# A macaron layer on one core: where the chunk matrix is stored, who stores the state-space parameters, and how long a gated tile's turn waits

## The chip, the cores and the metric

The kernel runs on 1 core of one Trainium2 chip. The metric is the time of one execution on the device in microseconds (us). A core has a TensorE (PE) that multiplies matrices, a VectorE (DVE), a ScalarE (ACT) and a GpSimd (POOL) for elementwise work, and a SyncE (SP) that here only issues transfers. Transfers can be issued by SP, ACT and POOL, and are carried by 16 DMA engines.

## What is computed

One layer of a decoder trunk on 256 tokens of width 2048, in float32: a SwiGLU block of hidden width 5632 with half weight, then a mixer (dilated window attention beside a state-space model, S5, of 64 groups of 16 channels with 64 complex states each), then a second SwiGLU block.

```
for l in range(DEPTH):
    h = h + 0.5 * swiglu_ffn(rms_norm(h, ffn1_norm[l]), ffn1_w_gate[l], ffn1_w_up[l], ffn1_w_down[l])
    proj = rms_norm(h, mix_norm[l]) @ w_in[l]          # q | k | v | u
    attn = mixture_of_dilations(q, k, v, rel_bias)
    y = s5_ssm(u, ssm_lambda_re[l], ..., ssm_d[l])
    y = jax.nn.gelu(y)
    y = y * jax.nn.sigmoid(y @ glu_w[l] + glu_b[l])
    h = h + jnp.concatenate([attn, y], axis=-1) @ w_out[l]
    h = h + 0.5 * swiglu_ffn(rms_norm(h, ffn2_norm[l]), ffn2_w_gate[l], ffn2_w_up[l], ffn2_w_down[l])
```

The S5 recurrence is run in chunks of 8 tokens. Four sets of matrices, which depend on the parameters alone, are worked out while the first SwiGLU block runs: the chunk matrix `m1` (inputs of a chunk to its state), `m2` (state to outputs), `k` (one row of Toeplitz blocks) and from it `t` (inputs of a chunk to its outputs).

## The kernel before

**The weights.** All large products run in `run` (L252). A pass is one block of 512 output columns of a weight; a group of a pass is 512 rows of it, 1 MB, loaded by SP into one of three `raw` buffers (L273). Each group is split in two halves, and each half into a high part `wh` (ACT, L286) and a low part `wl` (DVE, L291), in four buffers each. One **step** is the 12 matmuls of 128x512 on one half (L330 to L332), after which `step()` lets every running generator go on to its next `yield`. So a step is the clock of all other work: a `yield n` waits n steps. Each engine and each queue carries out its instructions in the order in which they were written. The split written at a step is the one for three steps later, and a weight's load is written when a `raw` buffer has been split.

**The gated tile.** The first block has 11 tiles of 512 hidden columns, each a pass over `w_gate` and one over `w_up`, 8 steps each, and then four passes over `w_down`. When the two passes of a tile are done, ACT and DVE have made `silu(gate) * up` (L363, L374) in `sil`, tokens on partitions. It has to stand with hidden columns on partitions. `by_blocks` (L129) does this turn: DVE transposes blocks of 32x32 (L134), after a step SP stores them to DRAM (`h_d`, L137), after two more SP loads them back from there (L140, four loads of 32 partitions), and after `yield 3` the caller splits the tile with ACT (L124) and DVE (L125) into `hid`, which the `w_down` passes read.

**The parameters.** `ssm_prepare` (L422) is a generator beside the first block. After the recurrence's powers and coefficients it loops over four pieces `pc` of 16 groups each. For a piece it writes `m1t` (in `s4a`) and `wk` (in `slot3`) by eight calls of `powers` (L649), each three DVE instructions with a scratch `tmp2` in `s4b` (L655 to L657). Then POOL stores `wk` to `m2_d` in one transfer of 1 MB (L667), DVE transposes `m1t` into `m1o`, all of `s4b` (L670), POOL stores it to `m1_d` in one transfer of 1 MB (L673), PE makes `k` with 16 small matmuls (L679), and SP stores `k` with 4 transfers (L688) and copies it to `t_d`, DRAM to DRAM, with 8 (L691). The next piece follows at once. The buffers serve as `hid` tiles 5 to 10 later, so the turn of tile 5 and those after it wait until `ssm_prepare` has ended, and the gate pass of tile 7 does not begin before.

**The mixer.** Its first two passes make `u`. When the first is done, `u_done(0)` (L962) calls `load_m1` (L698), which writes 16 loads of `m1_d`, 256 KB to 32 partitions each, on SP's queue, one after another.

Of the kernel before, what the change touches and what calls it, by code (L numbers as in the profile page):

```python
# [16 lines left out]
P = 128  # L17
# [29 lines left out]
def hybrid_layer_kernel(  # L47
# [80 lines left out]

    def by_blocks(src, dst):  # L129
        turns[0] += 1  # L130
        b = const.tile([P, 4, NT, P], F32, name=nm("blocks"), tag="blocks")
        hd = h_d[turns[0] % 2]
        for t in range(NT):
            vec.transpose(out=b[:, :, t].rearrange("p j (k c) -> p j k c", k=4),  # L134
                          in_=src[:, t, :].rearrange("p (k j c) -> p j k c", k=4, j=4))
        yield
        sync.dma_start(out=hd.rearrange("j p x -> p j x"), in_=b.rearrange("p j t x -> p j (t x)"))  # L137
        yield 2
        for j in range(4):
            sync.dma_start(out=dst[32 * j:32 * j + 32].rearrange("r (i x) -> r i x", i=4),  # L140
                           in_=hd[j].rearrange("(i r) x -> r i x", i=4))
        yield 3
        return dst.rearrange("p (i t x) -> p i t x", i=4, t=NT)
# [194 lines left out]
    def ffn(norm, w_gate, w_up, w_down, done, first):  # L338
# [31 lines left out]
        def up_done(c):  # L370
            def f(acc):
                a = sil.pop(c)
                for t in range(NT):
                    vec.scalar_tensor_tensor(out=a[:, t, :], in0=acc[t], scalar=norm.scale(t),  # L374
                                             in1=a[:, t, :], op0=ALU.mult, op1=ALU.mult)
# [12 lines left out]
            return f  # L388
# [33 lines left out]
    def ssm_prepare():  # L422
# [23 lines left out]
        pool.dma_start(out=dpad[:, :, 0:16], in_=ssm_d[0].rearrange("(j q c) -> q j c", j=4, q=16))  # L446
        zer = s2a[:, 0:8 * 112].rearrange("p (t x) -> p t x", t=8)
        pool.memset(zer, 0.0)
# [3 lines left out]

        def expo(xa, new, res_):
            xc, n, f, e, p2, ex, em = (new() for _ in range(7))
# [111 lines left out]
        ptab = a3[:, 2816:3840].rearrange("p (k s g) -> p k s g", k=8, s=2)  # L566
        tmp2 = s4b[:, 1536:2048]
        coef = a3[:, 0:128].rearrange("p (s g) -> p s g", s=2)
# [50 lines left out]
        for v, dst in ((0, cs), (64, csw)):  # L619
            for hb in range(2):  # L620
# [4 lines left out]
                for i in range(4):  # L625
# [3 lines left out]
                                   func=AF.Copy, scale=sgn)  # L629
                yield  # L630
        ps = tps()
# [5 lines left out]
        vec.tensor_tensor(out=dmask, in0=dmask, in1=ident[:, 96:112], op=ALU.add)  # L637
        yield

# [3 lines left out]
        wk = a3[:, 0:2304].rearrange("p (g r c) -> p g r c", r=9, c=16)  # L643
        ko = a3[:, 2304:2816].rearrange("p (q x) -> p q x", q=4)
        for pc in range(4):
            gs = slice(16 * pc, 16 * pc + 16)
            es = slice(256 * pc, 256 * pc + 256)

            def powers(dst, k, n, z, sz, down=False):  # L649

                pr, pi = (ptab[:, k - 1:k - 1 + n, v, gs][:, ::-1 if down else 1].rearrange("p k g -> p g k")
                          .unsqueeze(3).broadcast_to([P, 16, n, 16]) for v in range(2))
# [4 lines left out]
                vec.tensor_tensor(out=dst, in0=dst, in1=t_, op=ALU.add)  # L657

            act.activation(out=m1t[:, :, 7, :], in_=g3(bb[:, es]), func=AF.Copy)
            act.activation(out=wk[:, :, 0, :], in_=g3(cs[:, es]), func=AF.Copy)  # L660
            for k in range(1, 9, 2):
                n = 2 if k < 7 else 1
                powers(m1t[:, :, 8 - k - n:8 - k, :], k, n, bb, sb, True)
                yield
                powers(wk[:, :, k:k + 2, :], k, 2, cs, csw)
                yield
            pool.dma_start(out=m2_d[pc].rearrange("p (g x) -> p g x", g=16),  # L667
                           in_=wk[:, :, 1:9, :].rearrange("p g r c -> p g (r c)"))
# [4 lines left out]
            pool.dma_start(out=m1_d[pc].rearrange("j p x -> p j x"), in_=m1o)  # L673
            yield
            ps = tps()
            for q in range(4):
                for j in range(4):
                    g = 16 * pc + 4 * q + j
                    pe.matmul(ps[32 * j:32 * j + 32, q * P:(q + 1) * P], s2a[:, 16 * g:16 * g + 32],  # L679
                              wk[:, 4 * q + j, 0:8, :].rearrange("p r c -> p (r c)"), start=True, stop=True)  # L680
            yield
            act.activation(out=ko, in_=ps.rearrange("p (q x) -> p q x", q=4), func=AF.Copy)
            for q in range(4):
                vec.scalar_tensor_tensor(out=ko[:, q, 0:16], in0=dmask, scalar=dcol[:, 4 * pc + q:4 * pc + q + 1],
                                         in1=ko[:, q, 0:16], op0=ALU.mult, op1=ALU.add)
            for j in range(4):
                dst = k_d.rearrange("(q j) c x -> j c q x", j=4)[j, :, 4 * pc:4 * pc + 4, 112:240]
                sync.dma_start(out=dst, in_=ko[32 * j:32 * j + 16])  # L688
            yield 2
            for r in range(CH):  # L690
                sync.dma_start(out=t_d[pc, 16 * r:16 * r + 16].rearrange("c (g x) -> c g x", g=16),  # L691
                               in_=k_d[16 * pc:16 * pc + 16, :, (7 - r) * 16:(7 - r) * 16 + P]
                               .rearrange("g c x -> c g x"))


    mx = {}

    def load_m1():  # L698
        r3 = slot("slot3")
        mx["ring"] = [slot("s2a"), slot("s2b"), r3[:, 0:2048], r3[:, 2048:4096]]  # L700
        for pc in range(4):
            for j in range(4):
                sync.dma_start(out=mx["ring"][pc][32 * j:32 * j + 32].rearrange("r (i x) -> r i x", i=4),
                               in_=m1_d[pc, j].rearrange("(i r) x -> r i x", i=4))

# [6 lines left out]
    def ssm_run():  # L712
# [248 lines left out]
    def mixer(norm, out_done):  # L961
        def u_done(n):  # L962
            def f(acc):
                if n == 0:
# [106 lines left out]
    with tc.manual_schedule():  # L1071
# [143 lines left out]
```

## Time and profile before

| | |
|---|---|
| time, three runs | 1836.66 us median (1832.95 to 1837.66) |
| the profiled execution | 1833.54 us, of which the span 1831.8 us |
| TensorE matmul busy | 1798.0 us of the span |
| VectorE busy | 1060.3 us |
| ScalarE busy | 834.7 us |
| DMA | 401.23 MB, mean 219 GB/s |

The span is what the profiler recorded from the first to the last instruction; the rest of the execution's time lies around it. Times "at 190 us" are counted from the span's start. In a row of a timeline an engine's idle time and what ended it stand in brackets. A matmul's recorded duration is its way through a pipeline: in an undisturbed stretch one of 128x512 starts every 0.23 us though its row says 0.39.

### The profile page before, as it was taken

Reading aid. Unit: us, or ns where it says so; the run is one execution under the profiler, and the core shown is the slowest. Engines: PE = TensorE matmul, PEld = TensorE weight load, DVE = VectorE, ACT = ScalarE, POOL = GpSimd, SP = SyncE. Lnnn points to the kernel's source line nnn. Section 1 sums busy time; section 2 is a strip of 40 time slices with the busy share of each in tenths; the row PEclk is TensorE's granted clock in tenths of the full one; section 3 lists DMA queues with packets and bytes.
Section 4 is the critical chain, followed back from the end, with each engine's and each line's share of the span. In section 5 each row is a group of like instructions: output and inputs, shape, how many; then the busy total and the mean of one; then the engine's idle time right before and its main releaser. Section 6 shows DMA issues by size and latency. Waiting matters only on the chain.

```text
span 1831.8 us, 21467 instructions
## 1 busy us (share of the span) xinstructions
PE 1798.0 (98%) x8389; PEld 1476.9 (81%) x8389; DVE 1060.3 (58%) x1382; ACT 834.7 (46%) x1071; POOL 43.4 (2%) x91
## 2 busy tenths in 40 slices
PE   8999999999999999989999999999999999999999
PEld 6788777788888888868878888888888888888887
DVE  4778788555554555534795665555555555544443
ACT  5444344444444444435667555444444444443332
POOL 2100000000000000010000001000000000000000
PEclk8999999999999999989999999999999999999999
DMA  8665788867776666599656586677767767665662
GB/s 270 208 213 191 254 264 283 262 211 213 224 218 215 209 219 216 186 255 302 186 156 250 197 246 212 195 232 217 224 212 217 219 210 225 208 222 202 202 211 103
DMA packets 220389, 401.23 MB, mean 219 GB/s; under 512 B 9580, under 2 KB 50133, under 8 KB 219136
## 3 DMA queue, kind: packets, MB, share of 16 engines
q1 hardware_dynamic: 214384, 383.29, 65.7%
q0 software_dynamic: 4080, 13.43, 2.4%
q10 hardware_dynamic: 1824, 3.15, 0.7%
q8 instruction: 65, 1.06, 0.2%
q14 instruction: 36, 0.29, 0.0%
HBM read 370.00 MB, written 32.45 MB: 220 GB/s over the span
## 4 chain that ended last, share of the span: by engine, by line
PE 84%; DVE 8%; DMA 5%; ACT 1%; issue 1%; SPq 1%; ACTq 0%; DVEq 0%
PE acc L330 27%; PE acc L331 27%; PE acc L332 27%; DVE wl L291 3%; DMA h_d<-blocks 2%; DMA sil<-h_d 1%; DMA raw<-in_ffn_w_gate_dram 1%; DVE s4b L655 1%; ACT wh L286 1%; DMA raw<-in_w_in_dram 1%; DVE s1a L768 1%; DVE s1a L769 0%; DVE slot L656 0%; DVE s4a L657 0%; DVE s4a L656 0%
## 5 line engine op out<-in xcount | busy, mean ns | idle before, releaser
L291 DVE TENSOR_TENSOR wl<-raw,wh 128x1024 fp32r<-128x1024 f32 x628 | 764.6, 1225 | 635.0 <-ACT wh L286 634.5
L286 ACT ACTIVATE wh<-raw 128x1024 fp32r<-128x1024 f32 (+1 forms) x636 | 666.2, 1057 | 820.6 <-PE acc L332 762.5
L330 PE MATMUL acc<-wh,xth 128*128 128x512 f32 x1664 | 658.7, 396 | 16.5 <-ACT wh L286 16.5
L331 PE MATMUL acc<-wl,xth 128*128 128x512 f32 x1664 | 653.9, 393 | 3.6 <-DVE wl L291 3.2
L332 PE MATMUL acc<-wh,xtl 128*128 128x512 f32 x1664 | 652.0, 392 | 0.0
L330 PEld LDWEIGHTS acc<-wh,xth 128*128 128x128 f32 x1664 | 314.9, 189 | 85.1 <-ACT wh L286 19.0
L331 PEld LDWEIGHTS acc<-wl,xth 128*128 128x128 f32 x1664 | 315.0, 189 | 74.0 <-DVE wl L291 9.7
L332 PEld LDWEIGHTS acc<-wh,xtl 128*128 128x128 f32 x1664 | 314.8, 189 | 66.1
L331 PE MATMUL acc<-wl,hid 128*128 128x512 f32 x704 | 274.0, 389 | 0.0
L330 PE MATMUL acc<-wh,hid 128*128 128x512 f32 x704 | 274.0, 389 | 0.0
L332 PE MATMUL acc<-wh,hid 128*128 128x512 f32 x704 | 273.9, 389 | 0.0
L331 PEld LDWEIGHTS acc<-wl,hid 128*128 128x128 f32 x704 | 132.1, 188 | 27.5
L332 PEld LDWEIGHTS acc<-wh,hid 128*128 128x128 f32 x704 | 132.1, 188 | 27.5
L330 PEld LDWEIGHTS acc<-wh,hid 128*128 128x128 f32 x704 | 132.1, 188 | 27.3
L125 DVE TENSOR_TENSOR hid<-sil,hid 128x512 fp32r<-128x512 f32 x44 | 28.5, 688 | 79.6 <-ACT hid L124 79.6
L124 ACT ACTIVATE hid<-sil 128x512 fp32r<-128x512 f32 x44 | 25.4, 624 | 99.4 <-DMA sil<-h_d 99.4
L374 DVE SCALAR_TENSOR_TENSOR sil<-acc,rstd,sil 128x512 f32<-128x512 f32 x44 | 30.8, 741 | 0.0
L363 ACT ACTIVATE sil<-acc,rstd 128x512 f32<-128x512 f32 x44 | 27.5, 674 | 3.8 <-POOL rel L1114 3.8
L134 DVE STREAM_TRANSPOSE blocks<-sil 128x512 f32<-128x512 f32 x44 | 28.5, 685 | 0.0
L118 POOL TENSOR_TENSOR rs_t<-rstd 128x2 f32<-128x2 f32 x9 | 5.7, 632 | 659.8 <-DVE rstd L115 659.3
L330 PE MATMUL acc<-wh,slot 128*128 128x512 f32 x48 | 18.9, 393 | 0.0
L331 PE MATMUL acc<-wl,slot 128*128 128x512 f32 x48 | 18.7, 389 | 0.0
(324 smaller groups left out, 791.0 us busy)
## 6 DMA issues: line engine op xcount, KB each, us to landing
raw<-in_ffn_w_up_dram SPq DMA_DIRECT2D x88, 1024.0 KB, 5.9
raw<-in_ffn_w_down_dram SPq DMA_DIRECT2D x88, 1024.0 KB, 5.1
raw<-in_ffn_w_gate_dram SPq DMA_DIRECT2D x87, 1024.0 KB, 5.9
raw<-in_w_in_dram SPq DMA_DIRECT2D x32, 1024.0 KB, 5.6
raw<-in_w_out_dram SPq DMA_DIRECT2D x16, 1024.0 KB, 5.6
h_d<-blocks SPq DMA_DIRECT2D x28, 512.0 KB, 7.0
sil<-h_d SPq DMA_DIRECT2D x88, 128.0 KB, 7.3
m_d<-slot POOLq DMA_DIRECT2D x4, 1024.0 KB, 7.0
```

What stands on the lines that cost most here:

```text
L124: act.activation(out=h, in_=src, func=AF.Copy)
L125: vec.tensor_tensor(out=l, in0=src, in1=h.bitcast(F32), op=ALU.subtract)
L134: vec.transpose(out=b[:, :, t].rearrange("p j (k c) -> p j k c", k=4), in_=src[:, t, :].rearrange("p (k j c) -> p j k c", k=4, j=4))
L286: act.activation(out=h[:, c], in_=src[:, c], func=AF.Copy)
L291: vec.tensor_tensor(out=l, in0=src, in1=h.bitcast(F32), op=ALU.subtract)
L330: pe.matmul(acc[t], sh[:, c], h[:, kk, :], start=first, stop=False)
L331: pe.matmul(acc[t], sh[:, c], l[:, kk, :], start=False, stop=False)
L332: pe.matmul(acc[t], sl[:, c], h[:, kk, :], start=False, stop=last)
L363: act.activation(out=sil[c][:, t, :], in_=acc[t], func=AF.Silu, scale=norm.scale(t))
L374: vec.scalar_tensor_tensor(out=a[:, t, :], in0=acc[t], scalar=norm.scale(t), in1=a[:, t, :], op0=ALU.mult, op1=ALU.mult)
L655: vec.tensor_tensor(out=t_, in0=zb, in1=pr, op=ALU.mult)
L768: vec.tensor_tensor(out=tm, in0=a8, in1=prev.unsqueeze(1).broadcast_to([P, 2, 2, NG]), op=ALU.mult)
```

## The change

**The turn.** `by_blocks` gets a parameter `pause`, 3 by default; the gated tiles give 6. So ACT's and DVE's split of the turned tile is written three steps later.

**The stores.** They go into a list, `stores`. `beat()` is a `yield` that first issues one of them on POOL's queue (two where the first is one of `t`); `flush(tag)` issues what is left up to the last of a kind before its source is written anew. `m1` and `m2` are stored in four pieces of 256 KB, `k` in one transfer of 128 partitions (so `k_d` has 32 rows a group, of which 16 are read), `t` in eight as before. `m1`'s powers now come first, then its transposes, then the powers of `wk`, with empty steps among them: a piece takes 16 steps instead of 14. Some `yield`s ahead of the loop go, so that it begins at step 36 instead of 45, and `ssm_prepare` ends at step 108 instead of 101. The scratch of `powers` is a PSUM buffer instead of `tmp2`.

**The chunk matrix.** `m1_d` has the layout of the buffer that it is loaded into, so a piece is one load of 128 partitions, 8 KB each; its rows are in ascending powers, and `ssm_run` reads `um` backwards (`um[:, ::-1]`) to fit. The four loads are written one behind each of four weights, from the second group of `w_in`'s first pass on.

```diff
-    m1_d = dram.tile([4, 4, P, 512], F32, name="m1_d", tag="m1_d")
+    m1_d = dram.tile([4, P, 2048], F32, name="m1_d", tag="m1_d")
-    k_d = dram.tile([NG, 16, 15 * 16], F32, name="k_d", tag="k_d")
+    k_d = dram.tile([NG, 32, 15 * 16], F32, name="k_d", tag="k_d")
...
-    def by_blocks(src, dst):
+    def by_blocks(src, dst, pause=3):
...
-        yield 3
+        yield pause
...
-                    turned = yield from by_blocks(a, a.rearrange("p t x -> p (t x)"))
+                    turned = yield from by_blocks(a, a.rearrange("p t x -> p (t x)"), 6)
...
+        stores = []
+        def later(tag, dst, src):
+            stores.append((tag, dst, src))
+        def beat():
+            for _ in range(2 if stores and stores[0][0] == "t" else 1):
+                if stores:
+                    pool.dma_start(out=stores[0][1], in_=stores[0][2])
+                    del stores[0]
+            yield
+        def flush(tag):
+            while any(e[0] == tag for e in stores):
+                pool.dma_start(out=stores[0][1], in_=stores[0][2])
+                del stores[0]
...
-                t_ = tmp2[:, 0:256 * n].rearrange("p (g k c) -> p g k c", g=16, k=n)
+                t_ = tps()[:, 0:256 * n].rearrange("p (g k c) -> p g k c", g=16, k=n)
...
             for k in range(1, 9, 2):
                 n = 2 if k < 7 else 1
-                powers(m1t[:, :, 8 - k - n:8 - k, :], k, n, bb, sb, True)
-                yield
-                powers(wk[:, :, k:k + 2, :], k, 2, cs, csw)
-                yield
-            pool.dma_start(out=m2_d[pc].rearrange("p (g x) -> p g x", g=16),
-                           in_=wk[:, :, 1:9, :].rearrange("p g r c -> p g (r c)"))
+                powers(m1t[:, :, k:k + n, :], k, n, bb, sb)
+                yield from beat()
+                if k in (1, 5):
+                    yield from beat()
+            flush("m1")
             for j in range(4):
                 vec.transpose(out=m1o[:, j].rearrange("p (g c) -> p g c", c=32), in_=m1f[:, :, 32 * j:32 * j + 32])
                 if j % 2:
-                    yield
-            pool.dma_start(out=m1_d[pc].rearrange("j p x -> p j x"), in_=m1o)
-            yield
+                    yield from beat()
+            for i in range(4):
+                later("m1", m1_d[pc].rearrange("(j r) (i x) -> i r j x", r=32, i=4)[i], m1o[32 * i:32 * i + 32])
+            flush("m2")
+            act.activation(out=wk[:, :, 0, :], in_=g3(cs[:, es]), func=AF.Copy)
+            for k in range(1, 9, 2):
+                powers(wk[:, :, k:k + 2, :], k, 2, cs, csw)
+                yield from beat()
+                if k != 3:
+                    yield from beat()
+            for i in range(4):
+                later("m2", m2_d[pc].rearrange("p (i g x) -> i p g x", i=4, g=4)[i],
+                      wk[:, 4 * i:4 * i + 4, 1:9, :].rearrange("p g r c -> p g (r c)"))
...
-            for j in range(4):
-                dst = k_d.rearrange("(q j) c x -> j c q x", j=4)[j, :, 4 * pc:4 * pc + 4, 112:240]
-                sync.dma_start(out=dst, in_=ko[32 * j:32 * j + 16])
-            yield 2
+            later("k", k_d.rearrange("(q j) c x -> (j c) q x", j=4)[:, 4 * pc:4 * pc + 4, 112:240], ko)
+            k4 = k_d[16 * pc:16 * pc + 16]
             for r in range(CH):
-                sync.dma_start(out=t_d[pc, 16 * r:16 * r + 16].rearrange("c (g x) -> c g x", g=16),
+                later("t", t_d[pc, 16 * r:16 * r + 16].rearrange("c (g x) -> c g x", g=16),
...
-    def load_m1():
-        r3 = slot("slot3")
-        mx["ring"] = [slot("s2a"), slot("s2b"), r3[:, 0:2048], r3[:, 2048:4096]]
-        for pc in range(4):
-            for j in range(4):
-                sync.dma_start(out=mx["ring"][pc][32 * j:32 * j + 32].rearrange("r (i x) -> r i x", i=4),
-                               in_=m1_d[pc, j].rearrange("(i r) x -> r i x", i=4))
+    def load_m1(pc):
+        if pc == 0:
+            r3 = slot("slot3")
+            mx["ring"] = [slot("s2a"), slot("s2b"), r3[:, 0:2048], r3[:, 2048:4096]]
+        sync.dma_start(out=mx["ring"][pc], in_=m1_d[pc])
...
+        at = sum(len(p.ks) for p in ff1) // 1
+        def extra(n):
+            load_x(n)
+            if 0 <= n - at - 6 < 4:
+                load_m1(n - at - 6)
```

On ACT the first place is the gated tile 2 (its buffer is `hid_1125` before and `hid_1158` now), at the end of the gate pass of tile 3. Before, its split (L124) stands right behind the split of the weight half that is written at step 57, ahead of the `silu` of tile 3:

```order
L286 ACTIVATE wh_1600<-raw_1485 128x1024
L682 ACTIVATE slot_63_420<-tp_1583 128x512
L124 ACTIVATE hid_1125<-sil_494 128x4x128 x2
L363 ACTIVATE sil_494<-acc_1394,rstd_137 128x512
L363 ACTIVATE sil_494<-acc_1395,rstd_137 128x512
L286 ACTIVATE wh_1631<-raw_1485 128x1024
```

Now three more weight halves and the `silu` come first:

```order
L286 ACTIVATE wh_1635<-raw_1522 128x1024
L363 ACTIVATE sil_494<-acc_1421,rstd_137 128x512
L363 ACTIVATE sil_494<-acc_1422,rstd_137 128x512
L286 ACTIVATE wh_1659<-raw_1522 128x1024
L286 ACTIVATE wh_1681<-raw_1569 128x1024
L286 ACTIVATE wh_1701<-raw_1569 128x1024
L689 ACTIVATE slot_63_420<-s2b_419 128x16x16
L124 ACTIVATE hid_1158<-sil_494 128x4x128 x2
L286 ACTIVATE wh_1729<-raw_1619 128x1024
```

What moved is the split L124, from step 57 to step 60.

On SP the second place is the end of the first piece, around the load of the turned tile 2 (`sil_494<-h_d_107`). Before, `k` and `t` stand between the weights:

```order
L140 DMA sil_494<-h_d_107 32x4x256 x4
L273 DMA raw_1569<-in_ffn_w_gate_dram 128x4x512
L688 DMA k_d<-slot_63_420 16x4x128 x4
L273 DMA raw_1635<-in_ffn_w_gate_dram 128x4x512
L691 DMA t_d<-k_d 256x1x128 x8
L273 DMA raw_1682<-in_ffn_w_gate_dram 128x4x512
```

Now only weights and the turn are left there, and POOL's queue has for a piece what its own rows show, one row per kind:

```order
L651 DMA m_d<-s4b_422 32x4x512 x4
L651 DMA m_d<-slot_63_420 128x4x128 x4
L651 DMA k_d<-slot_63_420 128x4x128
L651 DMA t_d<-k_d 256x1x128 x8
L651 DMA m_d<-s4b_422 32x4x512 x4
```

So 12 issues a piece moved from SP to POOL's queue, and POOL's two large ones became eight.

On SP the third place is the start of the mixer; `raw` buffers hold groups of `w_in`. Before:

```order
L273 DMA raw_5743<-in_w_in_dram 128x4x512
L703 DMA s2a_5782<-m_d 32x4x512 x4
L703 DMA s2b_5783<-m_d 32x4x512 x4
L703 DMA slot_847_5781<-m_d 32x4x512 x8
L273 DMA raw_5809<-in_w_in_dram 128x4x512
```

and now, from two weights earlier on:

```order
L273 DMA raw_5690<-in_w_in_dram 128x4x512
L725 DMA s2a_5693<-m_d 128x2048
L273 DMA raw_5757<-in_w_in_dram 128x4x512
L725 DMA s2b_5694<-m_d 128x2048
L273 DMA raw_5792<-in_w_in_dram 128x4x512
L725 DMA slot_857_5692<-m_d 128x2048
L273 DMA raw_5840<-in_w_in_dram 128x4x512
L725 DMA slot_857_5692<-m_d 128x2048
L273 DMA raw_5875<-in_w_in_dram 128x4x512
```

What moved is that a weight now stands behind each 1 MB of `m1`, where the ninth weight of the mixer (`raw_5809`) stood behind all four.

More of the change, by code (lines that the diff above doesn't have):

```diff
@@ L446, in ssm_prepare @@
         pool.dma_start(out=dpad[:, :, 0:16], in_=ssm_d[0].rearrange("(j q c) -> q j c", j=4, q=16))
-        zer = s2a[:, 0:8 * 112].rearrange("p (t x) -> p t x", t=8)
+        zer = s2a[:, 0:16 * 112].rearrange("p (t x) -> p t x", t=16)
         pool.memset(zer, 0.0)
@@ L451, in ssm_prepare, with expo @@
         yield 3
-        def expo(xa, new, res_):
+        def expo(xa, new, res_, quick=False):
             xc, n, f, e, p2, ex, em = (new() for _ in range(7))
@@ L463, in expo @@
                               op0=ALU.logical_shift_left)
-            yield
+            if not quick:
+                yield
             vec.tensor_scalar(out=e, in0=f, scalar1=1.0 / math.factorial(8), scalar2=None, op0=ALU.mult)
@@ L468, in expo @@
                                          op0=ALU.add, op1=ALU.mult)
-            yield
+            if not quick:
+                yield
             vec.scalar_tensor_tensor(out=ex, in0=e, scalar=1.0, in1=p2, op0=ALU.add, op1=ALU.mult)
@@ L501, in ssm_prepare @@
         got = []
-        yield from expo(ldt, newcol, got)
+        yield from expo(ldt, newcol, got, True)
         dt = got[0]
@@ L566, in ssm_prepare @@
         ptab = a3[:, 2816:3840].rearrange("p (k s g) -> p k s g", k=8, s=2)
-        tmp2 = s4b[:, 1536:2048]
         coef = a3[:, 0:128].rearrange("p (s g) -> p s g", s=2)
@@ L584, in ssm_prepare @@
             vec.tensor_tensor(out=q1, in0=u1, in1=u2, op=ALU.add)
-            yield
+            if n > 1:
+                yield
         for o in range(2):
@@ L629, in ssm_prepare @@
                                    func=AF.Copy, scale=sgn)
-                yield
         ps = tps()
@@ L637, in ssm_prepare @@
         vec.tensor_tensor(out=dmask, in0=dmask, in1=ident[:, 96:112], op=ALU.add)
-        yield
         m1t = s4a.rearrange("p (g r c) -> p g r c", r=8, c=16)
@@ L644, in ssm_prepare @@
         ko = a3[:, 2304:2816].rearrange("p (q x) -> p q x", q=4)
+        stores = []
[6 more added lines that the diff above has]
+                    del stores[0]
+            yield
+        def flush(tag):
+            while any(e[0] == tag for e in stores):
+                pool.dma_start(out=stores[0][1], in_=stores[0][2])
+                del stores[0]
         for pc in range(4):
@@ L657, in powers @@
                 vec.tensor_tensor(out=dst, in0=dst, in1=t_, op=ALU.add)
-            act.activation(out=m1t[:, :, 7, :], in_=g3(bb[:, es]), func=AF.Copy)
-            act.activation(out=wk[:, :, 0, :], in_=g3(cs[:, es]), func=AF.Copy)
+            act.activation(out=m1t[:, :, 0, :], in_=g3(bb[:, es]), func=AF.Copy)
             for k in range(1, 9, 2):
                 n = 2 if k < 7 else 1
-                powers(m1t[:, :, 8 - k - n:8 - k, :], k, n, bb, sb, True)
-                yield
-                powers(wk[:, :, k:k + 2, :], k, 2, cs, csw)
-                yield
-            pool.dma_start(out=m2_d[pc].rearrange("p (g x) -> p g x", g=16),
-                           in_=wk[:, :, 1:9, :].rearrange("p g r c -> p g (r c)"))
+                powers(m1t[:, :, k:k + n, :], k, n, bb, sb)
[3 more added lines that the diff above has]
+            flush("m1")
             for j in range(4):
@@ L680, in ssm_prepare @@
                               wk[:, 4 * q + j, 0:8, :].rearrange("p r c -> p (r c)"), start=True, stop=True)
-            yield
+            yield from beat()
+            flush("k")
             act.activation(out=ko, in_=ps.rearrange("p (q x) -> p q x", q=4), func=AF.Copy)
@@ L685, in ssm_prepare @@
                                          in1=ko[:, q, 0:16], op0=ALU.mult, op1=ALU.add)
-            for j in range(4):
-                dst = k_d.rearrange("(q j) c x -> j c q x", j=4)[j, :, 4 * pc:4 * pc + 4, 112:240]
-                sync.dma_start(out=dst, in_=ko[32 * j:32 * j + 16])
-            yield 2
+            later("k", k_d.rearrange("(q j) c x -> (j c) q x", j=4)[:, 4 * pc:4 * pc + 4, 112:240], ko)
+            k4 = k_d[16 * pc:16 * pc + 16]
             for r in range(CH):
-                sync.dma_start(out=t_d[pc, 16 * r:16 * r + 16].rearrange("c (g x) -> c g x", g=16),
-                               in_=k_d[16 * pc:16 * pc + 16, :, (7 - r) * 16:(7 - r) * 16 + P]
-                               .rearrange("g c x -> c g x"))
+                later("t", t_d[pc, 16 * r:16 * r + 16].rearrange("c (g x) -> c g x", g=16),
+                      k4[:, 0:16, 16 * r:16 * r + P].rearrange("g c x -> c g x"))
+        while stores:
+            yield from beat()
     mx = {}
-    def load_m1():
-        r3 = slot("slot3")
-        mx["ring"] = [slot("s2a"), slot("s2b"), r3[:, 0:2048], r3[:, 2048:4096]]
-        for pc in range(4):
-            for j in range(4):
-                sync.dma_start(out=mx["ring"][pc][32 * j:32 * j + 32].rearrange("r (i x) -> r i x", i=4),
-                               in_=m1_d[pc, j].rearrange("(i r) x -> r i x", i=4))
+    def load_m1(pc):
[3 more added lines that the diff above has]
+        sync.dma_start(out=mx["ring"][pc], in_=m1_d[pc])
     def load_y(pc):
@@ L724, in ssm_run @@
             o = bt[:, 4 * b:4 * b + 4, :].rearrange("p q (r c) -> p q r c", r=CH)
-            i_ = um[:, :, 64 * b:64 * b + 64].rearrange("p r (q c) -> p q r c", q=4)
+            i_ = um[:, ::-1, 64 * b:64 * b + 64].rearrange("p r (q c) -> p q r c", q=4)
             if b % 2:
@@ L973, in f @@
                         load_bias(h)
-                    load_m1()
                 raw = mx["qk"][:, 1024 * n:1024 * n + 1024].rearrange("p (t x) -> p t x", t=NT)
@@ L1158, in load_x @@
                 sync.dma_start(out=res[n], in_=xin[:, :, n * 512:(n + 1) * 512])
-        run(ff1 + mixp + ff2, load_x, start)
+        at = sum(len(p.ks) for p in ff1) // 1
[3 more added lines that the diff above has]
+                load_m1(n - at - 6)
+        run(ff1 + mixp + ff2, extra, start)
 def _bias_rows():
```

6 lines of the change are left out of this document (2 added, 4 removed).

## Prediction

> **What bounds the kernel now.** I read the page first, then counts of matmuls by window, then the waits of the stretches that count too few.
>
> ```profile
> span 1831.8 us, 21467 instructions
> PE 1798.0 (98%) x8389; PEld 1476.9 (81%) x8389; DVE 1060.3 (58%) x1382; ACT 834.7 (46%) x1071; POOL 43.4 (2%) x91
> ```
>
> TensorE is the bound, but 98% busy says little, since recorded matmuls overlap. What counts is how many start. The next rows are windows of the one line L330, a third of the big matmuls: duration, busy time and count, granted clock, DMA share, GB/s.
>
> ```profile
> 400.00:800.00 400.00, 228.30 (x587) 1.00 0.67 213
> 140.70:354.15 213.45, 112.04 (x280) 0.98 0.78 251
> 809.95:825.30 15.35, 4.23 (x8) 0.67 0.98 295
> ```
>
> From 400 to 800 us, where nothing disturbs, one L330 takes 400 / 587 = 0.681 us, so a step (four of them) takes 2.73 us. The second window holds the four parameter pieces, steps 42 to 111: 280 x 0.681 = 190.8 us of work in 213.45, so **22.6 us are lost**. The third is two steps in the mixer: 8 x 0.681 = 5.45 us in 15.35, so **9.9 us are lost**. These two stretches are all that I expect the change to reach, out of the profiled execution's 1833.54 us.
>
> Not all of the first can go: the 16 small matmuls for `k`, four times, are real work. The chain of waits has the last of them (with their weight loads):
>
> ```profile
> 313.54 1.01 PE tp L679 x32
> ```
>
> 4 x 1.01 = 4.0 us stay, so 18.6 us at most are stalls. Who is waited for, by PE and then by ACT in that window (total, times, longest):
>
> ```profile
> PE acc L330 <- ACT wh L286: 5.4, 4, 2.8
> PE acc L331 <- DVE wl L291: 2.7, 4, 0.8
> ...
> ACT hid L124 <- DMA sil<-h_d: 29.7, 5, 9.9
> ACT wh L286 <- DMA raw<-in_ffn_w_up_dram: 12.4, 4, 4.9
> ACT wh L286 <- DMA raw<-in_ffn_w_gate_dram: 9.3, 3, 4.7
> ```
>
> PE's recorded idle time, 5.4 + 2.7 = 8.1 us, is under half of the 18.6; the rest is slow matmuls behind each gap, as the next rows show. PE waits for a weight half, and ACT, which makes it, had been standing in front of the turned gated tile. Tile 2, in order of time on DVE, SP, ACT and PE:
>
> ```profile
> 172.73 1.30 DVE L134 STREAM_TRANSPOSE blocks<-sil 128x512 f32<-128x512 f32 x2
> ...
> 175.57 0.51 SPq L137 DMA_DIRECT2D h_d<-blocks  x1
> 182.85 2.32 SPq L140 DMA_DIRECT2D sil<-h_d  x4
> 186.00 5.86 SPq L688 DMA_DIRECT2D k_d<-slot  x4
> 198.41 0.39 SPq L273 DMA_DIRECT2D raw<-in_ffn_w_gate_dram  x1
> 199.00 5.20 SPq L691 DMA_DIRECT2D t_d<-k_d  x8
> ...
> 193.88 1.15 ACT L124 ACTIVATE hid<-sil 128x512 fp32r<-128x512 f32 x2 [9.95 <-DMA sil<-h_d]
> ...
> 197.18 0.80 PE L330 MATMUL acc<-wh,xth 128*128 128x512 f32 x1 [2.81 <-ACT wh L286]
> ...
> 200.00:205.00 5.00, 5.00 (x16) 3.92 (x15) 4.93 (x8) 1.63 (x2) 0.00 (x0) 0.61 1.02 339
> ```
>
> ACT stood 9.95 us. PE had three halves in hand, some 8 us, and then ran dry; behind the gap the granted clock was 0.61, so 16 matmuls started in 5 us where 22 would.
>
> **Part 1, the turn and the stores.** From the end of the transposes (172.73 + 1.30 = 174.0) to the tile's arrival (193.9) is 19.9 us. Before, the split is written 1 + 2 + 3 = 6 steps behind the transposes, 6 x 2.73 = 16.4 us; with six for three it is 9 steps, 24.5 us. This is the worst of the five waits: of 9.95 us, 8.2 go by the three steps alone, and the others (29.7 - 9.95 = 19.75 over four, 4.9 each) go entirely. What is late next are the weights: ACT's 12.4 + 9.3 = 21.7 us on `raw`, at most 4.9 at a time. That is less than the 8 us that PE has in hand, if no other wait is added to it.
>
> The 12 issues a piece that leave SP's queue are these (shortest, median, longest in ns):
>
> ```profile
> L691 SPq DMA_DIRECT2D t_d<-k_d x32: 520/607/1227, 199.0 to 332.0; - x32
> L688 SPq DMA_DIRECT2D k_d<-slot x16: 303/433/1573, 186.0 to 320.8; - x16
> ```
>
> 32 x 0.607 + 16 x 0.433 = 26.4 us of SP's time, and in the timeline above weights queued behind them. I count this as part of the same 18.6 us. POOL gets 4 x (4 + 4 + 1 + 8) = 68 issues for its 8, of
>
> ```profile
> L667 POOL DMA_DIRECT2D m_d<-slot x4: 1121/1122/1174, 177.6 to 309.8; - x4
> L673 POOL DMA_DIRECT2D m_d<-s4b x4: 771/774/791, 182.0 to 314.4; - x4
> ```
>
> 0.77 to 1.12 us each, 52 to 76 us over 63 steps (172 us): hidden, because POOL has no other work there. The added wait is `t` on `k`'s landing; behind it on POOL stand only stores. Who waits for those: DVE for `m1o` (issued by step 47, written anew at 58, 30 us later), and ACT and DVE for `wk` (issued by step 54, written at 60, 16 us later). Landings of `raw` and of these 1 MB stores take 5 to 10 us.
>
> On DVE the scratch in PSUM: 64 instructions (32 calls, one write and one read) touch PSUM instead of SBUF. The nearest rows are one with a PSUM operand and one without, same size:
>
> ```profile
> L374 DVE SCALAR_TENSOR_TENSOR sil<-acc,rstd,sil 128x512 f32<-128x512 f32 x8 | 5.6, 738 | 0.0
> ...
> L657 DVE TENSOR_TENSOR slot<-slot,s4b 128x512 f32<-128x512 f32 x16 | 11.1, 692 | 0.6
> L291 DVE TENSOR_TENSOR wl<-raw,wh 128x1024 fp32r<-128x1024 f32 x70 | 84.1, 1214 | 21.7 <-ACT wh L286 21.6
> L125 DVE TENSOR_TENSOR hid<-sil,hid 128x512 fp32r<-128x512 f32 x10 | 6.5, 688 | 21.1 <-ACT hid L124 21.1
> ```
>
> 46 ns x 64 = 2.9 us at the most likely; 0 at the low end, double at the high end, as I have no row of a write. DVE's idle time there, 21.7 + 21.1 us, hides either, and spreading eight calls over 16 steps for 14 gives it 2 x 2.73 = 5.5 us more a piece. The earlier start and the dropped `yield`s move work among steps whose DVE is not full; I cost them at nothing.
>
> Bounds for part 1: 0 (another wait takes over) to 18.6. I take **15**, nearer to the upper end, because the wait that leads to PE's stalls is removed by its own length and 3.6 is left for late weights.
>
> A rule of the Trainium skill speaks against the pieces (DMA: Bandwidth & Descriptors, Bandwidth): transfers should be batched to 1 MiB or more. By the page's fit of 2.0 us + bytes / 436e3 I estimate 2.6 us for 256 KB, so 10.4 for four where one of 1 MB takes 4.4. By it the sum would stay as it is, since 10 us are within the 16 and 30 us above; this trace has 9.3 and 7.0 us for the whole stores, and none for a piece.
>
> **Part 2, the chunk matrix's loads.**
>
> ```profile
> 788.50 2.40 SPq L703 DMA_DIRECT2D s2a<-m_d  x4
> 791.08 6.45 SPq L703 DMA_DIRECT2D s2b<-m_d  x4
> 801.94 4.66 SPq L703 DMA_DIRECT2D slot<-m_d  x8
> 807.61 18.74 SPq L273 DMA_DIRECT2D raw<-in_w_in_dram  x5
> ...
> 818.28 2.00 ACT L286 ACTIVATE wh<-raw 128x1024 fp32r<-128x1024 f32 x2 [15.21 <-DMA raw<-in_w_in_dram]
> ...
> 819.39 0.79 PE L330 MATMUL acc<-wh,xth 128*128 128x512 f32 x1 [6.54 <-ACT wh L286]
> ...
> 805.00:810.00 5.00, 5.00 (x24) 4.14 (x23) 0.00 (x0) 0.00 (x0) 0.00 (x0) 1.00 1.07 222
> 815.00:820.00 5.00, 0.61 (x1) 0.29 (x1) 0.64 (x1) 1.72 (x2) 0.00 (x0) 0.50 1.05 384
> ```
>
> The next weight was issued only at 807.61, behind 4.2 MB that moved at 222 GB/s with all DMA engines busy; weights alone then moved at 384. ACT waited 15.21 us for it, and PE lost the 9.9. Now a weight stands behind each 1.05 MB. Two groups' worth, 2.1 MB, must move in 5.45 us for four groups: at 384 GB/s 5.46 us, no delay; at 222 GB/s 9.45, so 4.0 late each time, 16 in all. A `raw` is issued some 2.5 groups (13.6 us) before its split and lands in under 6, so 8 us are spare, and PE's 8 in hand make 16: even the slow end only just reaches PE. Saving between 5 and 9.9; I take **9**, near the end at 384, because the loads now go to 128 partitions as the weights do.
>
> **Sum.** 1833.54 - 15 - 9 = 1809.5; I say **1810**. The profiled execution is 3.1 us under the median of the three runs (1836.66), so a median may also come out some 3 us higher.
>
> **The rivals.**
>
> *One term only* (0.20). The stores still move the same bytes beside the weights, and ACT's waits for `raw` (21.7 us, which the change does not address) grow into the slack that the turn leaves. Then part 1 gives 0 to 7 and the time is 1817.5 to 1824.5; if instead the mixer's stall only moves to a later weight, 1833.5 - 15 = 1818.5. For it: those waits exist. Against: each is under 5 us. The Trainium skill bears on this (DMA: Bandwidth & Descriptors, SWDGE vs HWDGE vs iDMA, "Issuing engines are not separate DMA queues"): another issuing engine saves only the issue time. If that is all the stores' move brings, part 1 rests on the turn's three steps alone; the trace shows the DMA share at 1.02 and 1.07 in the rows above, which agrees that the engines are shared.
>
> *It does not do what it says* (0.08). The turned tile lands later by as much as its split is later, as its load queues behind other traffic, and the weights behind 1 MB loads are as late as behind 4 MB. Then all stays within 1828 to 1839. Against: SP's queue at the turn holds less than before, not more.
>
> *Slower* (0.09). `m1`'s stores are now the thin transfers, 32 partitions each, as its loads were, at 222 GB/s. If they hold up everything beside them, the parameter stretch becomes DMA-bound. It moved 251 GB/s x 213.45 us = 53.6 MB; at 222 that takes 241 us, 28 more than now, and with the mixer's 9 saved the time is 1853. It decides at 53.6 MB / (213.45 + 9) = 241 GB/s: below that mean rate the kernel loses. Against: only 4.2 of the 53.6 MB are thin, and the rest has 384 GB/s.
>
> **How the numbers follow.** The forecast has 0.63, within 1804 to 1815: all of 18.6 and 9.9 gained is 1805, less 0.6 for the lowest of the three runs. The range reaches up over most of the first rival to the mixer alone (1833.5 - 9.9 = 1823.6) plus 3 for the median: 1804 to 1827. Left out are the other two, 0.17. About 0.3% (5.5 us) is what a measurement of this kernel can tell from no change. The forecast and one-term cases are faster by more than that: 0.83; no effect 0.08; slower 0.09.
>
> **What would show it.** Right: in the window of the parameter pieces no ACT wait for `sil<-h_d` over 2 us and no PE gap behind it, L330 at one per 0.69 us there; POOL issuing through steps 44 to 107; at the mixer's start no ACT wait for `raw` of 15 us and a clock that stays at 1.00. Wrong: ACT waiting for `raw` instead, over 8 us at a time; DVE's idle time gone in that window; ACT or DVE waiting for `m_d` stores before they write `wk` or `m1o`; a DMA rate near 222 GB/s while the stores run.

## The result, and the profile after

| | before | after |
|---|---|---|
| median, device us | 1836.78 | 1806.53 |
| profiled execution, us | 1833.54 | 1805.77 |
| its span, us | 1831.8 | 1804.0 |
| ratio (95% interval) | | 0.9841 (0.9824 to 0.9858) |

The change makes the kernel 1.6% faster. The page's head, and the windows of L330 that answer to those shown of before (duration, busy time and count, granted clock, DMA share, GB/s); the second window is again steps 42 to 111, the third steps 279 and 280:

```profile
span 1804.0 us, 21475 instructions
PE 1785.0 (99%) x8389; PEld 1472.8 (82%) x8389; DVE 1064.4 (59%) x1382; ACT 841.1 (47%) x1071; POOL 78.4 (4%) x151
...
400.00:780.00 380.00, 216.90 (x558) 1.00 0.68 220
141.00:336.30 195.30, 109.38 (x280) 1.00 0.85 278
791.50:796.95 5.45, 3.11 (x8) 1.00 0.74 255
```

The same 280 matmuls of L330 take 195.3 us instead of 213.45, and the eight in the mixer 5.45 instead of 15.35: 18.1 and 9.9 us, 28.0 together, where the two profiled executions differ by 27.8. The clock is 1.00 in both. What is left in the first stretch over 280 x 0.681 = 190.8 us is the four groups of small matmuls for `k`. In that stretch the waits of PE have no row at all, and of ACT's two rows neither is a transfer:

```profile
ACT wh L286 <- PE acc L332: 103.3, 68, 2.3
ACT wh L286 <- DVE hid L125: 3.3, 2, 1.7
```

The turn of tile 2 on DVE, SP and ACT (start, duration, instruction, idle time before it):

```profile
167.99 1.30 DVE L134 STREAM_TRANSPOSE blocks<-sil 128x512 f32<-128x512 f32 x2
...
171.15 0.98 SPq L137 DMA_DIRECT2D h_d<-blocks  x1
180.34 2.02 SPq L140 DMA_DIRECT2D sil<-h_d  x4
...
192.67 1.14 ACT L124 ACTIVATE hid<-sil 128x512 fp32r<-128x512 f32 x2
```

ACT takes the tile without any idle time before it. And DVE has done the transposes at 169.3, while step 51 began at 165.5 (at 165.8 before, when they were done at 174.0): **3.8 us into the step instead of 8.2**. This second difference turned out to matter too.

The start of the mixer, on SP's queue, and two windows of the core (PE, weight loads, DVE, ACT, POOL, clock, DMA share, GB/s):

```profile
759.52 0.34 SPq L725 DMA_DIRECT2D s2a<-m_d  x1
764.17 0.37 SPq L273 DMA_DIRECT2D raw<-in_w_in_dram  x1
764.75 0.34 SPq L725 DMA_DIRECT2D s2b<-m_d  x1
769.60 0.37 SPq L273 DMA_DIRECT2D raw<-in_w_in_dram  x1
...
775.00:780.00 5.00, 5.00 (x24) 4.14 (x23) 3.18 (x3) 2.12 (x2) 0.00 (x0) 1.00 1.02 408
780.00:785.00 5.00, 5.00 (x24) 4.14 (x23) 2.01 (x3) 2.12 (x2) 0.00 (x0) 1.00 1.04 415
```

In these two windows weights and the chunk matrix move together at 408 and 415 GB/s, where the thin loads moved at 222. The other windows of 5 us from 760 to 790 have 363, 401, 282 and 372. SP waits there only for a free `raw` buffer, 28.4 us in six waits, and no weight comes late.

### The profile page after: what moved, and what is told of

Its sections match the earlier page's. It is cut to its first block, busy times and chain, and to the rows that moved or that the text cites. A ratio compares the mean times of both kernels' runs of the same rounds, so it can differ in the third digit from the quotient of the medians.

```text
span 1804.0 us, 21475 instructions
## 1 busy us (share of the span) xinstructions
PE 1785.0 (99%) x8389; PEld 1472.8 (82%) x8389; DVE 1064.4 (59%) x1382; ACT 841.1 (47%) x1071; POOL 78.4 (4%) x151
## 4 chain that ended last, share of the span: by engine, by line
PE 94%; DVE 3%; DMA 1%; ACT 1%; issue 0%; SPq 0%; ACTq 0%
PE acc L330 30%; PE acc L332 30%; PE acc L331 30%; DVE wl L291 1%; DMA raw<-in_ffn_w_gate_dram 1%; DVE s1a L789 1%; DVE s1a L790 0%; DVE slot L791 0%; ACT wh L286 0%; PE tp L800 0%; PE tp L702 0%; PE tp L765 0%; PE tp L331 0%; PE tp L330 0%; PE tp L332 0%
## 5 line engine op out<-in xcount | busy, mean ns | idle before, releaser
L330 PE MATMUL acc<-wh,xth 128*128 128x512 f32 x1664 | 654.3, 393 | 4.4 <-ACT wh L286 4.4
L330 PEld LDWEIGHTS acc<-wh,xth 128*128 128x128 f32 x1664 | 313.0, 188 | 70.3 <-ACT wh L286 4.9
L330 PE MATMUL acc<-wh,hid 128*128 128x512 f32 x704 | 273.9, 389 | 0.0
L330 PEld LDWEIGHTS acc<-wh,hid 128*128 128x128 f32 x704 | 132.2, 188 | 27.5
L374 DVE SCALAR_TENSOR_TENSOR sil<-acc,rstd,sil 128x512 f32<-128x512 f32 x44 | 30.9, 743 | 0.0
L134 DVE STREAM_TRANSPOSE blocks<-sil 128x512 f32<-128x512 f32 x44 | 28.6, 687 | 0.0
L124 ACT ACTIVATE hid<-sil 128x512 fp32r<-128x512 f32 x44 | 25.0, 614 | 0.0
L651 POOL DMA_DIRECT2D t_d<-k_d x32 | 17.9, 579 | 23.4 <-DMA k_d<-slot 23.0
```

Of the source, the lines that this page charges most:

```text
L124: act.activation(out=h, in_=src, func=AF.Copy)
L330: pe.matmul(acc[t], sh[:, c], h[:, kk, :], start=first, stop=False)
L651: pool.dma_start(out=stores[0][1], in_=stores[0][2])
```

## The experiments

Times of stretches are taken between first matmuls of steps in each run's trace, which agree to 0.1 us where nothing differs. All in us; "turn" is the pause. The runs e3 and e4 change only the loads of the chunk matrix (e4 its layout too).

| run | turn | stores | steps 42 to 111 | steps 279, 280 | ratio to before (95%) |
|---|---|---|---|---|---|
| before | 3 | SP and POOL, whole | 213.5 | 15.4 | |
| the change | 6 | POOL, spread | 195.3 | 5.4 | 0.984 (0.982 to 0.986) |
| e1_pause3 | 3 | as the change | 196.6 | 5.4 | 0.985 (0.983 to 0.986) |
| e2_pause6_only | 6 | as before | 199.2 | 15.9 | 0.992 (0.990 to 0.994) |
| e3_burst_wide | 6 | as the change | 195.3 | 5.5 | 0.986 (0.985 to 0.988) |
| e4_thin_between | 6 | as the change | 195.3 | 9.8 | 0.986 (0.985 to 0.988) |
| e5_spread_on_sp | 3 | SP, spread | 195.3 | 5.4 | 0.985 (0.983 to 0.987) |
| e6_whole_at_once | 3 | POOL, bunched | 195.4 | 5.4 | 0.985 (0.983 to 0.987) |
| e7_kt_on_pool | 3 | as before, k and t on POOL | 214.3 | 14.6 | 0.999 (0.998 to 1.000) |
| e8_kt_on_pool_pause6 | 6 | as before, k and t on POOL | 196.9 | 15.5 | 0.991 (0.988 to 0.993) |
| e9_m1_at_the_turn | 3 | POOL, all beside the turn | 212.0 | 5.4 | 0.995 (0.993 to 0.997) |
| e10_sixteen_steps | 3 | as before | 208.8 | 15.6 | 0.999 (0.997 to 1.000) |
| e11_late_dve_pause3 | 3 | as the change | 201.1 | 5.4 | 0.988 (0.985 to 0.990) |
| e12_late_dve_pause6 | 6 | as the change | 195.3 | 5.4 | 0.985 (0.982 to 0.987) |

### The turn and the stores, one without the other

```diff
-                    turned = yield from by_blocks(a, a.rearrange("p t x -> p (t x)"), 6)
+                    turned = yield from by_blocks(a, a.rearrange("p t x -> p (t x)"), 3)
```

> The changed kernel with the turn's pause back at 3 steps. Turn theory (the three steps are what removes the stall): ACT waits for sil<-h_d again, and at least 8 of the 18.1 us that the parameter stretch (steps 42 to 111) gained come back, so some 1815 us or more. Stores theory (the stores' move and spreading remove it, since the tile lands earlier): the traces of the change put the landing of tile 2 at about 188 us and step 57 on ACT at 184, so ACT waits some 4 us a tile, under the 8 us that PE has in hand, and less than 2 us come back: 1806 to 1809 us.

1.25 us came back, as the stores theory forecast. ACT waits again, 15.4 us in all, but PE does not run dry, save at one tile:

```profile
ACT hid L124 <- DMA sil<-h_d: 15.4, 4, 6.4
ACT wh L286 <- DMA raw<-in_ffn_w_gate_dram: 3.9, 2, 3.0
ACT wh L286 <- DMA raw<-in_ffn_w_up_dram: 3.3, 1, 3.3
PE acc L331 <- DVE wl L291: 0.8, 1, 0.8
```

So with the stores changed, the longer turn is worth 1.25 us. The other way round, `pause` 6 alone in the kernel before:

> The kernel before with 6 steps for the gated tile's turn and nothing else. Turn theory: at least 12 of the 18.1 us of the parameter stretch are gained, 1825 us or less, and the 9.9 us in the mixer stay. Stores theory: the waits for late weights (21.7 us on ACT) and the transfers of k and t between them on SP's queue stall PE all the same, at most 6 us are gained: 1831 us or more.

14.2 of the 18.1 us were gained. No wait for a turned tile is left, but the waits for weights grew from 21.7 to 52.2 us in the same stretch, and PE hardly felt them:

```profile
ACT wh L286 <- DMA raw<-in_ffn_w_gate_dram: 30.7, 11, 7.5
ACT wh L286 <- DMA raw<-in_ffn_w_up_dram: 21.5, 7, 4.8
PE acc L331 <- DVE wl L291: 1.3, 3, 0.8
PE acc L330 <- ACT wh L286: 0.3, 1, 0.3
```

Each half does most of the work alone: 16.9 and 14.2, together 18.1. The open question was what in the stores' half does it.

### Not the queue, and not the pieces

In e1's kernel, `beat` and `flush` issue on SP's queue:

```diff
-                    pool.dma_start(out=stores[0][1], in_=stores[0][2])
+                    sync.dma_start(out=stores[0][1], in_=stores[0][2])
```

> The changed kernel with the turn's pause at 3 (which lost 1.25 us in steps 42 to 111) and with all its stores issued on SP's queue instead of POOL's, same places, same pieces. Queue theory (weights no longer stand behind k, t and their waits on SP): SP waits for k's landing ahead of t and holds the weights, so 6 us or more come back in that stretch (195.3 us in the changed kernel, 213.5 before). Spreading theory (the pieces over 16 steps are what help): under 3 us come back.

Nothing came back, though SP waited 11.9 us for `k`'s landings: the queue theory failed. In e1's kernel again, bunched on POOL:

```diff
-            for _ in range(2 if stores and stores[0][0] == "t" else 1):
+            for _ in range({"t": 8, "m1": 4}.get(stores[0][0], 1) if stores else 1):
...
-            for i in range(4):
-                later("m2", m2_d[pc].rearrange("p (i g x) -> i p g x", i=4, g=4)[i], ...)
+            later("m2", m2_d[pc].rearrange("p (g x) -> p g x", g=16), ...)
```

> The changed kernel with the turn's pause at 3, stores on POOL's queue, but not spread: m2 in one transfer of 1 MB, the four pieces of m1 in one step, the eight of t in one step. Queue theory: under 2 us come back. Spreading theory: the turned tiles land later again, ACT waits 8 us or more for some, and 4 us or more come back in steps 42 to 111.

Nothing came back here either, against the spreading theory. And the kernel before with only the queue of `k` and `t` changed:

```diff
-                sync.dma_start(out=dst, in_=ko[32 * j:32 * j + 16])
+                pool.dma_start(out=dst, in_=ko[32 * j:32 * j + 16])
...
-                sync.dma_start(out=t_d[pc, ...
+                pool.dma_start(out=t_d[pc, ...
```

> The kernel before with the stores of k and t issued on POOL's queue instead of SP's, nothing else: pause 3, whole stores of m1 and m2, 14 steps a piece. Queue theory: 10 us or more of the 18.1 are gained in steps 42 to 111 (213.5 before). Spreading theory: at most 5, since the same bytes go out at the same steps and the turned tile of 20 us stays late. The mixer keeps its 9.9 us under both.

Nothing was gained: 214.3. ACT's waits for the turn stand much as before, 30.7 us for 29.7:

```profile
ACT hid L124 <- DMA sil<-h_d: 30.7, 5, 10.3
ACT wh L286 <- DMA raw<-in_ffn_w_up_dram: 8.4, 3, 3.6
PE acc L330 <- ACT wh L286: 7.4, 3, 3.2
```

> The kernel before with the turn's pause at 6 (which alone gained 14.2 us in steps 42 to 111, with ACT then waiting 52 us for weights) and k and t on POOL's queue. Queue theory: those waits for weights fall under 20 us and the stretch comes to 196 us or less. Spreading theory: they stay over 35 us and the stretch at 198 or more.

With `pause` 6 beside it the queue was worth 199.2 - 196.9 = 2.3 us, and ACT's waits for weights fell from 52.2 to 25.6: between the two forecasts. So the queue matters a little to the weights, and it does not bring the turned tile sooner. No run has SP's queue and whole stores together in the new places. Nor does a run separate the scratch in PSUM, which goes with the stores' half everywhere; in the kernel before, DVE waited for `m1`'s store ahead of the old scratch once, 1.7 us.

### When the bytes go out, and when DVE comes to the transposes

e6's kernel with the store of `m1` moved behind that of `m2`, so that both, `k` and `t` go out while the tile is turned:

```diff
-            for i in range(4):
-                later("m1", ...)
...
             later("m2", m2_d[pc].rearrange("p (g x) -> p g x", g=16), ...)
+            for i in range(4):
+                later("m1", ...)
```

> The changed kernel with the turn's pause at 3, whole stores, and m1's store held back from the steps after its transposes to those of m2's, so that 2 MB, k and t all go out between steps 51 and 57 of each tile, where its turn is stored and loaded; DVE's cadence of 16 steps stays. Timing theory (the stores no longer fall on the turn, so the tile lands in time): the longest ACT wait for sil<-h_d is 8 us or more again and 6 us or more come back in steps 42 to 111 (195.4 us without this). DVE theory (two more steps a piece leave DVE time, so that PE has its three halves in hand when ACT waits): under 3 us come back.

16.7 of the 18.1 us came back, with DVE's cadence as in the change. The longest wait is 7.9, just under the 8 forecast. Its tile 2:

```profile
168.69 1.30 DVE L134 STREAM_TRANSPOSE blocks<-sil 128x512 f32<-128x512 f32 x2
...
171.85 2.65 SPq L137 DMA_DIRECT2D h_d<-blocks  x1
178.12 0.37 SPq L273 DMA_DIRECT2D raw<-in_ffn_w_up_dram  x1
185.52 1.81 SPq L140 DMA_DIRECT2D sil<-h_d  x4
...
192.75 1.16 ACT L124 ACTIVATE hid<-sil 128x512 fp32r<-128x512 f32 x2 [7.39 <-DMA sil<-h_d]
```

The store to DRAM, issued at 171.85, let the load start only at 185.52, 13.7 us later, where the change needs 9.2. So the timing of the stores matters. But it is not all: the kernel before had 19.9 us from the transposes to the tile, e6 had 20.2, and e6 lost nothing. In the kernel before, two steps more in each piece, started two steps earlier (two `yield`s ahead of the loop are left out):

```diff
                 powers(wk[:, :, k:k + 2, :], k, 2, cs, csw)
-                yield
+                yield 2 if k in (3, 5) else 1
```

> The kernel before, starting the pieces two steps earlier and with two empty steps more in each, 16 for 14: every piece now stores m2 at step 53, m1 at 55, k at 57 and t at 59 of its tile, as the first did before (whose turn cost 6.4 us); pause 3, queues and buffers as before. DVE theory: the stretch of steps 42 to 111 (213.5 us) gains 10 us or more. Timing theory: the first piece's stall comes at each of three or four turns and the stretch is no shorter than 210 us.

4.7 us were gained, between the two: the first tile's stall went (0.5 for 6.4), those of the next two grew to 6.5 and 5.8. The kernel before has a fourth stall in this stretch, 4.2 us in steps 110 and 111, at the turn of tile 5; in e10 that turn begins at step 107 and loses 1.1 us outside the stretch, so most of the 4.7 is a stall that moved. DVE's place in the program, not the mere number of steps, had to be looked at. For the turns of tiles 2 to 4 I took the time from the start of its step (51, 67, 83) to the start of ACT's split, and what the two steps 9 and 10 later lost over 2 x 2.72 us:

| run, pause 3 | tile 2: tile at, lost | tile 3 | tile 4 |
|---|---|---|---|
| before | 28.1, 6.4 | 25.9, 2.0 | 25.9, 2.0 |
| e1 | 22.2, 0 | 23.6, 0 | 25.2, 1.2 |
| e5 | 21.7, 0 | 21.4, 0 | 21.3, 0 |
| e6 | 24.0, 0 | 23.4, 0 | 23.4, 0 |
| e7 | 28.5, 6.1 | 28.1, 6.3 | 26.8, 5.1 |
| e9 | 26.6, 4.2 | 28.1, 5.7 | 28.8, 6.8 |
| e10 | 24.5, 0.5 | 29.3, 6.5 | 28.2, 5.8 |

There is one border, between 24.0 and 24.5 us: 24.0 lost nothing, 24.5 lost 0.5, 25.2 lost 1.2 and 25.9 lost 2.0. The fourth stall of the kernel before fits too: its tile came 26.5 us after the start of step 101 and 4.2 were lost. The border can be counted. The half for step 60 is written at step 57 ahead of the tile's split; the first one that has to stand behind it is the half for step 61. That step begins 10 x 2.72 us after the turn's, plus 1.2 for the small matmuls of `k`, so 28.4, and its second matmul, which needs DVE's low part, 0.2 later. From the tile's arrival ACT needs 3.25 us for the two splits of the tile, the `silu` and this half, and DVE 1.2 more for the low part: 28.6 - 3.25 - 1.2 leaves 24.2. ACT's rows at tile 2 in e6, which came just in time (step 51 began at 165.9):

```profile
183.66 1.06 ACT L286 ACTIVATE wh<-raw 128x1024 fp32r<-128x1024 f32 x1 [1.66 <-PE acc L332]
189.94 1.15 ACT L124 ACTIVATE hid<-sil 128x512 fp32r<-128x512 f32 x2 [5.22 <-DMA sil<-h_d]
191.00 1.25 ACT L363 ACTIVATE sil<-acc,rstd 128x512 f32<-128x512 f32 x2
192.14 2.95 ACT L286 ACTIVATE wh<-raw 128x1024 fp32r<-128x1024 f32 x3
```

Up to the border ACT's wait costs nothing; beyond it each microsecond costs one or more, as PE runs dry and the granted clock falls (0.61 behind the gap of tile 2 before). Two things add up against it: DVE's lateness at the transposes, and the time from there to the tile's arrival. Before they were 8.2 + 19.9 for tile 2 and 9.8 + 16.1 for the next two; in e6 3.8 + 20.2, 7.1 + 16.3 and 6.1 + 17.3; in e9 3.8 + 22.8 for tile 2.

The last two kernels delay DVE. They do the two transposes of tiles 2 to 4 four times over, which gives the same tile after 3.7 us more of DVE's time:

```diff
-        for t in range(NT):
+        for t in list(range(NT)) * times:
```

> The changed kernel with the turn's pause at 3, and for tiles 2 to 4 of the first block DVE does the turn's two transposes four times over, the same result each time: six more of 0.61 us, 3.7 us more in front of the turn. Deadline theory (the split written at step 57 is the one that PE needs 9 steps, 24.5 us, after step 51 begins; DVE's lateness at the transposes and the transfers' time add up against it): with pause 3 alone ACT had the tiles at 22.2, 23.6 and 25.2 us after that, so now at 26, 27 and 29, and 5 us or more come back in steps 42 to 111 (196.6 us). Transfer theory (only how long the turn's transfers take counts, and it is what it was): under 2 us come back.

4.6 us came back against e1, between the two forecasts, and where the border says: ACT had the tiles at 23.5, 26.7 and 25.5 us, and 0, 4.0 and 1.6 us were lost. They were not as late as forecast (26, 27 and 29): DVE ended the transposes 3.6, 5.1 and 2.4 us later than in e1, but the way from there to the tile took 16.1 to 16.6 us where it had taken 18.4 to 18.6. So the two terms are not independent; why the way is shorter stays open. The same with `pause` 6:

> The changed kernel itself, pause 6, with the same 3.7 us of repeated transposes in front of the turns of tiles 2 to 4. Deadline theory: the deadline is 12 steps, 32.7 us, and the tiles are there at 27 or 28, so steps 42 to 111 stay at 195.3 us within 0.5. If DVE's time itself bounded the stretch, 3.7 us a tile would come back instead, some 8 to 11 us.

Nothing came back: 195.3. With six steps the first half behind the split is the one for step 64, which begins 36.6 us after the turn's step. By the same count, with the 2.5 us that ACT needs there, I estimate the border at 33 us; ACT had the tiles at 27.2, without a wait, and no run comes near it.

### The chunk matrix: width and place

All four wide loads at the end of the first pass, as the sixteen stood:

```diff
+                    for pc in range(4):
+                        load_m1(pc)
...
-            if 0 <= n - at - 6 < 4:
-                load_m1(n - at - 6)
```

> The changed kernel with its four loads of the chunk matrix (128 partitions, 1 MB each) written one after another where the sixteen stood, at the end of the mixer's first pass. Placing theory (a weight has to stand between them): the weight behind 4.2 MB is at least 11 us late at 384 GB/s, and 4 us or more of the 9.9 come back at steps 279 and 280. Width theory (the loads to 32 partitions at 222 GB/s were the trouble): under 1 us comes back.

Steps 279 and 280 kept their 5.4 us, so the forecast of the placing theory failed there. But 2.8 us came back a little later, in steps 281 to 299, where `u` for the state-space model is loaded after the burst; ACT waits 9.07 us for it where it waits 3.18 in the change:

```profile
816.61 1.15 ACT L748 ACTIVATE slot<-s1a 128x512 f32<-128x512 f32 x2 [9.07 <-DMA s1a<-u_d]
...
817.18 0.63 PE L757 MATMUL tp<-ident,slot 128*128 128x128 f32 x4 [2.59 <-DVE slot L750]
```

The old layout, 1 MB as four loads to 32 partitions, between the weights:

```diff
-        sync.dma_start(out=mx["ring"][pc], in_=m1_d[pc])
+        for j in range(4):
+            sync.dma_start(out=mx["ring"][pc][32 * j:32 * j + 32].rearrange("r (i x) -> r i x", i=4),
+                           in_=m1_d[pc, j].rearrange("(i r) x -> r i x", i=4))
```

> The changed kernel with the chunk matrix stored and loaded in the old layout (four loads of 32 partitions, 256 KB each, for each 1 MB), but still 1 MB behind each of four weights. Placing theory: under 1 us comes back in the mixer. Width theory: 222 GB/s makes each of four weights 4 us later, 16 us in all, so that ACT waits for weights 8 us or more and 1 to 8 us come back between steps 270 and 290.

4.4 us came back in steps 279 and 280 and 0.9 behind them. ACT waits, and the windows show why:

```profile
783.55 2.01 ACT L286 ACTIVATE wh<-raw 128x1024 fp32r<-128x1024 f32 x2 [3.98 <-DMA raw<-in_w_in_dram]
795.12 2.00 ACT L286 ACTIVATE wh<-raw 128x1024 fp32r<-128x1024 f32 x2 [9.56 <-DMA raw<-in_w_in_dram]
...
765.00:770.00 5.00, 5.00 (x24) 4.14 (x23) 2.45 (x2) 2.04 (x2) 3.78 (x11) 1.00 1.05 238
790.00:795.00 5.00, 4.80 (x22) 3.63 (x20) 0.00 (x0) 0.00 (x0) 0.00 (x0) 1.00 1.05 250
```

These two windows have 238 and 250 GB/s at a DMA share of 1.05, and two between them 281 at the same share; the change moved 401 and 408 from 765 to 770 and from 775 to 780, where e4 moved 238 and 281. The layouts differ in the length of a row too, 2 KB against 8 KB. But a weight's rows are also 2 KB, and weights alone moved at 384 in the kernel before, so rows of 2 KB alone do not make a load slow. Of the 9.9 us, width alone keeps 7.1 and place alone 4.7; it takes both for all.

## Why the prediction was right, step by step

- **The two stretches.** That all of the gain lies in steps 42 to 111 and 279 to 280, with 22.6 and 9.9 us over the bare matmuls there, held: 18.1 and 9.9 us were gained, and no other stretch of steps differs by more than 0.6 us.
- **Part 1, its size.** 15 was taken, of bounds 0 to 18.6; it is 18.1. The 3.6 left for late weights did not come: ACT's 21.7 us on `raw` went to none. They were not a fixed cost of the weights: 52.2 us in e2, 25.6 in e8, 9.5 in e6, 7.2 in e1, none in e5. What of the stores sets them no run separates.
- **Part 1, its cause.** The step that the turn's pause removes the wait by its own length held, and e2 shows it alone: 14.2, close to the 15. What failed is what stood beside it. SP's 26.4 us of issues were counted as a part of the same 18.6, but moving them in the kernel before gained nothing (e7), and moving them back lost nothing (e5). The Trainium skill (DMA: Bandwidth & Descriptors, SWDGE vs HWDGE vs iDMA) says that another issuing engine saves only the time to issue. These two runs agree: 195.3 on SP, 214.3 on POOL. And "I cost them at nothing" was wrong: the stores' half is worth 16.9 us with the old pause (e1), and since neither queue nor pieces explain it, the new times are left: DVE comes to tile 2's transposes 4.4 us sooner, and `m1`'s store is off the turn. Undoing the second brings 16.7 us back (e9), undoing about as much of the first 4.6 (e11). Since either half alone brings the tiles inside the border or close to it, the sum came out near without this term; that is luck.
- **PE's 8 us in hand.** At the turn it is less. In e6 ACT is ready for the split of tile 2 18.8 us after the start of step 51, so up to the border it may wait 5.2 to 5.7, since its own work behind the tile takes the rest. e6's wait of 5.22 us cost 0.06, e1's of 6.36 cost 1.25.
- **The scratch in PSUM.** 46 ns an instruction was taken, 0 to 92 the bounds. It is 0:

```profile
L670 DVE TENSOR_TENSOR tp<-s2b,slot 128x512 f32<-128x512 f32 x16 | 11.1, 693 | 0.0
L672 DVE TENSOR_TENSOR slot<-slot,tp 128x512 f32<-128x512 f32 x16 | 11.0, 688 | 0.6
```

  against 684 and 692 in SBUF. So the 738 of L374 is no measure for these; whether it comes from that operation or from its operands, no row separates.
- **POOL.** It did wait for `k` before `t`, 23.0 us in four times, and nobody waited for POOL, as said. The 1 MiB rule did not decide: spread pieces (e1) and bunched stores with `m2` whole (e6) give 196.6 and 195.4 with `pause` 3.
- **Part 2.** 9 was taken, it is 9.9. Width and place were both named, and the slow end, "only just reaches PE", is e4: it keeps 4.7 of the 9.9, just under the 5 taken as the least.
- **The rivals.** For the slower one the rate had to fall under 241 GB/s; it rose to 278. The time of "one term only" is what e2 shows, the pause alone with the old mixer: 1821.57 us median.
- **The sum.** 1809.5 against a profiled 1805.77: of the 3.7 between them, 3.1 are part 1 and 0.9 part 2, with 0.3 against it elsewhere.

## What to carry to other kernels

A late transfer costs nothing until it passes a border that can be counted in the program: how many steps after its issue the first instruction stands that the bound engine needs. Take off the work that the engines between still have to do. Add up against what is left everything from the step's start, the lateness of the engine that begins the chain as well as the transfers, and two cures that each bring the sum inside will not add. Where weights stream, load by all partitions and put a weight behind each megabyte of anything else.

## What was not expected of the hardware

- Loads of 256 KB to 32 partitions each kept the DMA share at 1.07 while 222 GB/s moved (before), and at 1.05 with weights between them while 238 to 281 moved (e4); with loads of 1 MB to 128 partitions between the same weights up to 415 moved at 1.04.
- A VectorE `TENSOR_TENSOR` of 128x512 in float32 takes as long with its output or one input in PSUM (693, 688 ns) as in SBUF (684, 692 ns).
